# Softmax times V on one core: a third split load, the check of the values between passes, and the verdict in the last pass alone

## The chip, the core and the metric

The kernel runs on one core of one Trainium2 chip. The core has a matrix engine (TensorE, PE in the profile, with its weight loads listed as PEld), a vector engine (VectorE, DVE), an activation engine (ScalarE, ACT), a general engine (GpSimd, POOL) and an engine that here only issues transfers (SyncE, SP). Sixteen DMA engines move data between HBM and the on-chip buffers. The metric is the device time of one execution in microseconds (us); less is better.

## What is computed

```python
# scores: (8, 12, 1024, 1024) float32, v: (8, 12, 1024, 64) float32
scores_max = np.max(scores, axis=-1, keepdims=True)
attn = np.exp(scores - scores_max)
attn = attn / (np.sum(attn, axis=-1, keepdims=True) + 1e-8)
return np.matmul(attn, v).astype(np.float32)
```

There are 96 heads. A head has a 1024x1024 matrix of scores (4.19 MB) and a 1024x64 matrix of values (0.26 MB), and gives a 1024x64 result (0.26 MB).

## The kernel before

**Passes.** A loop (L423) runs 24 times; the text counts these passes from 0 to 23. A pass takes four heads as two pairs, `k` = 0 and `k` = 1, with n0 = 4 times the number of the pass. A pair lies in one buffer of scores, `s_bufs[k]`, of 128 partitions by 16 "rows" `r` by 1024 float32: 8.39 MB. So there are 32 rows in a pass; the text numbers them 0 to 31 across both pairs.

**One row.** ACT takes the exponential without subtracting the maximum (L377), two rows in one instruction, or one row for the last eight rows of a pass (`late`), into one of eight float16 buffers `p_nat`. PE transposes the row in eight blocks (L390; called T0 to T31 here) into PSUM, in one of two buffers `psT` of two rows each. DVE copies the transposed rows back to SBUF: two rows at a time (L402, 128x2048; called p0 to p11 here), or one row (L398) for the last eight. PE multiplies the copied row with the values and with a column of ones (L152; F0 to F31), so that the sum of the row comes out beside the product. After three rows DVE takes the reciprocals of the sums into `seen` (L132) and multiplies (L140). The product of a row is put `LAG` = 3 rows behind its transposition (L409), and PE's order is fixed by hand (`in_line`).

**Values.** `v_sb` holds the values of four heads in float32. POOL spreads them into the float16 tile `vones` (L248): those of pair 0 after that pair's last product (L163), those of pair 1 at the end of the pass (`last`, L352).

**Checks.** Because the maximum is not subtracted, the kernel checks that the fast way was allowed. `watch_v` (L257) takes the largest magnitude of `vones` on DVE, once a pass, behind the copy of row 7 (L404), and folds it into `fits` (L269). `judge` (L281) runs at the end of each pass (L414): two small reductions fold `seen` (L285, L286), two small operations make `right` (L289, L292), PE counts the good partitions with one matmul (L297), and DVE writes `count` (L301). After the loop every engine reads `count` (L430), and if it is not 128 the slow `general` runs (L434). It does not run in the profiled execution.

**Transfers.** All are issued by SP on one queue, in an order fixed by hand (`queue`). A pass issues: the load of pair 0 of the next pass (`load_first`, L225: three conditional instructions, of which only the one for the whole pair runs, except in pass 22, where the two halves run), the store of pair 0 (L170), and then, in an arm of `last`, the load of pair 1 of the next pass (L219), the store of pair 1 and the load of the next values (L238). A load into a buffer of scores waits until ACT has read the rows that it overwrites. The load of pair 1 is one transfer of 8.39 MB in passes 0 to 21; in pass 22 it is cut into seven (4, 4, 3, 2, 1, 1, 1 rows). Pass 23 only stores its results (`end`, L180).

**`last`** (L347) is a set of branches on n0, which every engine executes, whether it has work in them or not.

Of the kernel before, what the change touches and what calls it, by code (L numbers as in the profile page):

```python
# [26 lines left out]
def kernel(  # L27
# [6 lines left out]
    nc = tc.nc  # L34
# [155 lines left out]

    stores = []
    writers, users = {}, {}
    watches = []

    def apart(a, b, reason="stores of two heads are disjoint"):
        tc.declare_no_dep(a.ins, b.ins, across_iterations=True, reason=reason)
# [47 lines left out]
    def spread_v(k):  # L244

        for t in range(T):
            for s in range(S):
                spread = nc.gpsimd.tensor_copy(  # L248
                    out=vones[s * Q : (s + 1) * Q, k, :, t, 0:D].rearrange(
                        "i (h l) d -> i h l d", l=L  # L250
                    ),
                    in_=v_sb[(k * T + t) * Q : (k * T + t + 1) * Q, :, s],
                )
                for watch in watches:
                    apart(spread, watch, "products in between")

    def watch_v(behind):  # L257

        watch = nc.vector.tensor_reduce(  # L259
            out=most,  # L260
            in_=vones[:, :, :, :, 0:D].rearrange("p k c t d -> p k (c t) d"),
            axis=mybir.AxisListType.XYZ,
            op=ALU.max,
            apply_absolute_value=True,
        )
        after(watch, behind)
        watches.append(watch)
        for bound, op in ((V_MIN, ALU.is_ge), (V_MAX, ALU.is_le)):
            nc.vector.scalar_tensor_tensor(  # L269
                out=fits, in0=most, scalar=bound, in1=fits, op0=op, op1=ALU.mult  # L270
            )
# [6 lines left out]
    most, fits, right = small("most"), small("fits"), small("right", FP16)  # L278
    nc.gpsimd.memset(fits, 1.0)

    def judge(bank):  # L281

        n = K * R
        part = small("part")
        nc.vector.tensor_reduce(out=seen[:, 0:1], in_=seen[:, 0 : n + 1], axis=X, op=ALU.min)  # L285
        nc.vector.tensor_reduce(  # L286
            out=seen[:, n + 1 : n + 2], in_=seen[:, 1 : n + 2], axis=X, op=ALU.max
        )
        nc.vector.scalar_tensor_tensor(  # L289
            out=part, in0=seen[:, n + 1 : n + 2], scalar=1.0, in1=fits, op0=ALU.is_le, op1=ALU.mult  # L290
        )
        nc.vector.scalar_tensor_tensor(  # L292
            out=right, in0=seen[:, 0:1], scalar=1.0 / SUM_MAX, in1=part, op0=ALU.is_ge, op1=ALU.mult
        )
        cell = bank[0:1, G * M : G * M + 1]
        in_line(
            nc.tensor.matmul(  # L297
                out=cell, lhsT=right[:], rhs=vones[:, 0, 0, 0, D : D + 1], start=True, stop=True
            )
        )  # L300
        nc.vector.tensor_copy(out=count[:], in_=cell)  # L301

    def general():

        s_rows = scores.rearrange("b h (r p) j -> (b h r) p j", p=P)
        v_rows = v.rearrange("b h (c p) d -> (b h) p c d", p=P)
        o_rows = out.rearrange("b h (r p) d -> (b h r) p d", p=P)
        row, p_row, pt = (s_bufs[0][:, r, :] for r in range(3))
        v1 = s_bufs[0][:, 3, 0 : C * (D + 1)].rearrange("p (c m) -> p c m", m=D + 1)
        out_row = s_bufs[0][:, 4, 0:D]  # L310
        lift, den = small("lift"), small("den")
        nc.gpsimd.memset(s_bufs[0][:, 3, 0 : C * (D + 1)], 1.0)
        half = SK // 2
        with tc.For_i(0, BH * C, 1, iteration_sync="reg_based") as n:
            nc.sync.dma_start(out=row, in_=s_rows[bass.ds(n, 1)].rearrange("o p j -> (o p) j"))
            nc.sync.dma_start(
                out=v1[:, :, 0:D], in_=v_rows[bass.ds(n // C, 1)].rearrange("o p c d -> (o p) c d")
            )
            nc.vector.tensor_reduce(out=lift, in_=row, axis=X, op=ALU.max, negate=True)
            nc.scalar.activation(out=p_row, in_=row, func=EXP, bias=lift[:])  # L320
            for c in range(C):
                at = c * P % half
                nc.tensor.transpose(
                    out=psO_bufs[c * P // half][:, at : at + P],
                    in_=p_row[:, c * P : (c + 1) * P],
                    identity=ident32[:],
                )
            for h in range(2):
                nc.scalar.copy(out=pt[:, h * half : (h + 1) * half], in_=psO_bufs[h][:, 0:half])
            for c in range(C):  # L330
# [12 lines left out]
            nc.sync.dma_start(  # L343
                out=o_rows[bass.ds(n, 1)].rearrange("o p d -> (o p) d"), in_=out_row
            )

    def last(n0):  # L347

        before = queued[-1:]
        k = K - 1  # L350
        with tc.If(n0 < BH - AHEAD) as cmp:
            spread_v(k)  # L352
            with tc.If(n0 < BH - 2 * AHEAD) as cmp2:
                queued[:] = before
                load(k, (n0 + (AHEAD + T * k)) % BH)
                store(n0, k)
                load_v((n0 + 2 * AHEAD) % BH)
            with cmp2.Else():
                queued[:] = before
                load(k, BH - T, (4, 4, 3))  # L360
                store(n0, k)
                load(k, BH - T, (2, 1, 1, 1), 11)
        with cmp.Else():
            queued[:] = before
            end()

    def heads(n0):

        for k in range(K):
            st = dict(psO=[take(psO_bufs) for g in range(GROUPS)])  # L370
            for r in range(R):
                late = k == K - 1 and r >= R // 2
                if r % EB == 0:
                    p_nat, psT2, pt2 = take(p_bufs), take(psT_bufs), take(pt_bufs)
                    rows = 1 if late else EB
                    for g in range(0, EB, rows):
                        exp = nc.scalar.activation(  # L377
                            out=p_nat[:, g : g + rows, :].rearrange(
                                "p r (x v) -> p x r v", v=Q * L
                            ),  # L380
                            in_=s_bufs[k][:, r + g : r + g + rows, :].rearrange(
                                "p r (i x l) -> p x (r i) l", i=Q, l=L
                            ),
                            func=EXP,
                        )
                        rewrite(p_nat, exp)
                p_row = p_nat[:, r % EB, :].rearrange("p (h q l) -> p h l q", q=P, l=L)
                psT, pt = psT2[:, r % EB, :], pt2[:, r % EB, :]
                for c in range(C):
                    turned = nc.tensor.transpose(  # L390
                        out=psT[:, c * P : (c + 1) * P],
                        in_=p_row[:, c // L, c % L, :],
                        identity=ident16[:],
                    )
                    in_line(turned)
                    other_bank(psT2, r % EB, turned)
                if late:
                    copy = nc.vector.tensor_copy(out=pt, in_=psT)  # L398
                    rewrite(pt2, copy)
                    other_bank(psT2, r % EB, copy)  # L400
                elif r % EB == EB - 1:
                    copy = nc.vector.tensor_copy(out=pt2[:], in_=psT2[:])  # L402
                    rewrite(pt2, copy)
                if k == 0 and r == R // 2 - 1:  # L404
                    watch_v(copy)
                if r == R - 1 and k < K - 1:
                    load_first(n0)
                pending.append((n0, k, r, pt, st))
                if len(pending) > LAG:  # L409
                    finish(pending.pop(0))  # L410
        while pending:
            finish(pending.pop(0))
        last(n0)
        judge(st["psO"][-1])  # L414

    assert BH % AHEAD == 0 and BH >= 2 * AHEAD and SK == Q * S * C and K == 2
    load_v(0)
    for k in range(K):
        load(k, T * k, (R // 2, R // 2) if k == 0 else (R,))
    for k in range(K):  # L420
        spread_v(k)
    load_v(AHEAD)
    with tc.For_i(  # L423
        0, BH, AHEAD, iteration_sync="reg_based"
# [41 lines left out]
```

## Time and profile before

| what | value |
|---|---|
| time, median of 3 runs | 1070.16 us (1069.1 to 1070.58) |
| the profiled execution | 1069.46 us |
| its span, first to last instruction | 1067.5 us |
| PE / DVE / ACT / POOL busy | 793.6 / 768.8 / 737.3 / 239.2 us |
| moved by DMA | 453.06 MB, mean 424 GB/s |
| packets of the one large queue | 98.6% of 16 engines' span |
| mean granted TensorE clock | 0.897 |

The profiled execution is 0.7 us below the median and 1.96 us above its own span. Busy time is an average over stretches with different limits: an engine that is busy for 74% of the span may still set the pace for a short stretch. All times of day below are in us from the start of the span. In the profile's groups, "PE psO <- vones,pt" is a product, "PE psT <- ident,p_nat" a transposition, "DVE pt <- psT" a copy; a wait is put down to the releaser that came last by the profile, and where that engine had long been done it was another.

### The profile page before, as it was taken

To read this page: it belongs to the slowest core of one execution; us is meant where nothing else is said; L and a number is where in the kernel's file an instruction comes from. 1 tells how busy PE (TensorE), PEld (TensorE's weight loads), DVE (VectorE), ACT (ScalarE), POOL (GpSimd) and SP (SyncE) were. 2 spreads that over 40 slices of the span, in tenths; PEclk is the share of its full clock that TensorE was granted. 3 is DMA by queue.
4 is the path that set the end of the run, shared out by engine and by line. 5 is a ranking of instruction groups with operands and counts; after the bars stand their busy time and mean duration, and the time that the engine had idled before them with its cause. 6 is when DMAs were issued, how large, how long until landed. Compare 5 with 4: busy or idle time off the path is not lost.

```text
span 1067.5 us, 32791 instructions
## 1 busy us (share of the span) xinstructions
PE 793.6 (74%) x12312; PEld 757.7 (71%) x12312; DVE 768.8 (72%) x1539; ACT 737.3 (69%) x504; POOL 239.2 (22%) x399
## 2 busy tenths in 40 slices
PE   2578768786786777867878668776786777866887
PEld 2578668686686776867768668776686777866877
DVE  1578767696686866867769667785686866867788
ACT  3567568666686576856867668667686586756893
POOL 3031131211311203113121131221311303113121
PEclk9889889898898988989989889898898988989899
DMA  9999999999999999999999999999999999999993
GB/s 393 441 438 413 422 462 413 452 413 431 453 413 452 426 419 449 417 433 446 440 425 449 425 423 452 413 428 456 413 452 413 431 453 413 452 410 434 432 429 151
DMA packets 18580, 453.06 MB, mean 424 GB/s; under 512 B 2064, under 2 KB 2192, under 8 KB 8720
## 3 DMA queue, kind: packets, MB, share of 16 engines
q1 hardware_dynamic: 18576, 452.99, 98.6%
q8 instruction: 4, 0.07, 0.0%
HBM read 637.53 MB, written 25.17 MB: 621 GB/s over the span
## 4 chain that ended last, share of the span: by engine, by line
DMA 58%; ACT 27%; issue 6%; PE 3%; PEld 2%; DVE 2%; ACTq 1%; SPq 0%; PEldq 0%; DVEq 0%
DMA s_nat<-in_scores_dram 58%; ACT p_nat L377 26%; PE psO L152 1%; PEld L390 1%; PE psT L390 1%; DVE pt L402 1%; PEld L152 1%; ACTq L377 1%; DVE most L259 0%; ACT L377 0%; DVE pt L398 0%; SPq L219 0%; ACTq L423 0%; DVE seen L132 0%; DVE out_sb L140 0%
## 5 line engine op out<-in xcount | busy, mean ns | idle before, releaser
L377 ACT ACTIVATE p_nat<-s_nat 128x2048 f16<-128x2048 f32 (+1 forms) x480 | 706.5, 1557 | 118.9 <-PE psO L152 42.5
L390 PE MATMUL psT<-ident,p_nat 128*128 128x128 f16 x6144 | 505.4, 232 | 166.2 <-ACT p_nat L377 166.2
L390 PEld LDWEIGHTS <-p_nat 128*128 128x128 f16 x6144 | 425.1, 118 | 176.0 <-ACT p_nat L377 176.0
L402 DVE COPY pt<-psT 128x2048 f16<-128x2048 f16 x288 | 352.4, 1224 | 261.5 <-PE L390 165.2
L152 PE MATMUL psO<-vones,pt 128*128 128x130 f16 x6144 | 486.6, 223 | 62.9 <-DVE fits L269 40.4
L152 PEld LDWEIGHTS <-pt 128*128 128x128 f16 x6144 | 387.8, 99 | 84.7 <-DVE pt L402 55.6
L248 POOL CAST vones<-v_sb 32x512 f16<-32x512 f32 x392 | 238.5, 608 | 813.4 <-PE psT L390 318.6
L140 DVE TENSOR_TENSOR out_sb<-psO,seen 64x192 f32<-64x192 f32 (+1 forms) x576 | 191.8, 333 | 18.0
L377 ACT ACT_TABLE_LOAD x24 | 30.8, 1283 | 195.4 <-DMA s_nat<-in_scores_dram 178.5
L398 DVE COPY pt<-psT 128x1024 f16<-128x1024 f16 x192 | 123.5, 685 | 2.3
L259 DVE TENSOR_REDUCE most<-vones 128x1 f32<-128x2048 f16 x24 | 54.9, 2286 | 0.7
L132 DVE RECIPROCAL seen<-psO 128x3 f32<-128x3 f32 (+1 forms) x288 | 49.3, 171 | 2.8 <-PE L390 1.4
L297 PE MATMUL psO<-vones,right 128*1 128x1 f16 x24 | 3.9, 164 | 41.0 <-DVE right L292 41.0
L297 PEld LDWEIGHTS <-right 128*1 128x1 f16 x24 | 1.9, 79 | 45.3 <-DVE right L292 45.3
L301 DVE CAST count<-psO 1x1 int32<-1x1 f32 x24 | 3.5, 146 | 6.2 <-PE psO L297 6.2
L269 DVE SCALAR_TENSOR_TENSOR fits<-most,fits 128x1 f32<-128x1 f32 x48 | 7.4, 155 | 0.0
L289 DVE SCALAR_TENSOR_TENSOR part<-seen,fits 128x1 f32<-128x1 f32 x24 | 5.3, 220 | 0.8
L285 DVE TENSOR_REDUCE seen<-seen 128x1 f32<-128x33 f32 x24 | 4.5, 188 | 0.8
L292 DVE SCALAR_TENSOR_TENSOR right<-seen,part 128x1 f16<-128x1 f32 x24 | 3.9, 162 | 0.8
L286 DVE TENSOR_REDUCE seen<-seen 128x1 f32<-128x33 f32 x24 | 4.2, 177 | 0.0
L77 DVE MEMSET vones<- 128x64 f16 x1 | 0.1, 112 | 0.8 <-PEq L450 0.8
L74 DVE CAST ident<-ident 128x128 f16<-128x128 f32 x1 | 0.2, 227 | 0.4 <-POOL ident masks.py:199 0.4
(8 smaller groups left out, 1.1 us busy)
## 6 DMA issues: line engine op xcount, KB each, us to landing
s_nat<-in_scores_dram SPq DMA_DIRECT2D x50, 4096.0 KB, 18.7
v_sb<-in_v_dram SPq DMA_DIRECT2D x24, 1024.0 KB, 22.2
out_dram<-out_sb SPq DMA_DIRECT2D x47, 512.0 KB, 16.8
s_nat<-in_scores_dram SPq DMA_DIRECT2D x2, 2048.0 KB, 22.8
s_nat<-in_scores_dram SPq DMA_DIRECT2D x1, 1536.0 KB, 27.5
s_nat<-in_scores_dram SPq DMA_DIRECT2D x3, 512.0 KB, 20.8
s_nat<-in_scores_dram SPq DMA_DIRECT2D x1, 1024.0 KB
s_nat<-in_scores_dram SPq DMA_DIRECT2D x47, 28.4
```

Of the source, the lines that this page charges most:

```text
L132: nc.vector.reciprocal(out=recip, in_=psO[:, :, D : D + 1])
L140: nc.vector.tensor_tensor(out=out_bufs[k][part, g * G : g * G + rows, :], in0=psO[part, :, t * N : t * N + D], in1=recip[part].to_broadcas ...
L152: product = nc.tensor.matmul(out=st["psO"][g][:, i * M : (i + 1) * M], lhsT=pt[:, c * P : (c + 1) * P], rhs=vones[:, k, c].rearrange("p t ...
L248: spread = nc.gpsimd.tensor_copy(out=vones[s * Q : (s + 1) * Q, k, :, t, 0:D].rearrange("i (h l) d -> i h l d", l=L), in_=v_sb[(k * T + t) ...
L259: watch = nc.vector.tensor_reduce(out=most, in_=vones[:, :, :, :, 0:D].rearrange("p k c t d -> p k (c t) d"), axis=mybir.AxisListType.XYZ, ...
L269: nc.vector.scalar_tensor_tensor(out=fits, in0=most, scalar=bound, in1=fits, op0=op, op1=ALU.mult)
L289: nc.vector.scalar_tensor_tensor(out=part, in0=seen[:, n + 1 : n + 2], scalar=1.0, in1=fits, op0=ALU.is_le, op1=ALU.mult)
L297: nc.tensor.matmul(out=cell, lhsT=right[:], rhs=vones[:, 0, 0, 0, D : D + 1], start=True, stop=True)
L377: exp = nc.scalar.activation(out=p_nat[:, g : g + rows, :].rearrange("p r (x v) -> p x r v", v=Q * L), in_=s_bufs[k][:, r + g : r + g + ro ...
L390: turned = nc.tensor.transpose(out=psT[:, c * P : (c + 1) * P], in_=p_row[:, c // L, c % L, :], identity=ident16[:],)
L398: copy = nc.vector.tensor_copy(out=pt, in_=psT)
L402: copy = nc.vector.tensor_copy(out=pt2[:], in_=psT2[:])
```

## The change

The check of the values reads `v_sb` (as loaded) in place of `vones`, and stands once before the loop and then in `last`, behind the second spreading, in the arm of passes 0 to 22. `judge` is cut in two: `fold`, the two small reductions, stays at the end of each pass ahead of `last`; the rest moves into the arm of the last pass. The load of pair 1 that pass 21 issues, for pass 22, is cut into two halves by one more branch. In the last two rows of a pass the products follow their transpositions one row closer. The slow `general` issues its transfers from ACT in place of SP.

```diff
-    def watch_v(behind):
-
-        watch = nc.vector.tensor_reduce(
+    def watch_v():
+
+        nc.vector.tensor_reduce(
             out=most,
-            in_=vones[:, :, :, :, 0:D].rearrange("p k c t d -> p k (c t) d"),
-            axis=mybir.AxisListType.XYZ,
+            in_=v_sb[:].rearrange("p h s l d -> p (h s l d)"),
+            axis=X,
             op=ALU.max,
             apply_absolute_value=True,
         )
-        after(watch, behind)
-        watches.append(watch)
...
-    def judge(bank):
+    def fold():
 
         n = K * R
-        part = small("part")
         nc.vector.tensor_reduce(out=seen[:, 0:1], in_=seen[:, 0 : n + 1], axis=X, op=ALU.min)
         nc.vector.tensor_reduce(
             out=seen[:, n + 1 : n + 2], in_=seen[:, 1 : n + 2], axis=X, op=ALU.max
         )
+
+    def judge(bank):
+
+        n = K * R
+        part = small("part")
...
-    def last(n0):
+    def last(n0, bank):
 
         before = queued[-1:]
         k = K - 1
         with tc.If(n0 < BH - AHEAD) as cmp:
             spread_v(k)
+            watch_v()
             with tc.If(n0 < BH - 2 * AHEAD) as cmp2:
-                queued[:] = before
-                load(k, (n0 + (AHEAD + T * k)) % BH)
-                store(n0, k)
-                load_v((n0 + 2 * AHEAD) % BH)
+                with tc.If(n0 < BH - 3 * AHEAD) as cmp3:
+                    queued[:] = before
+                    load(k, (n0 + (AHEAD + T * k)) % BH)
+                    store(n0, k)
+                    load_v((n0 + 2 * AHEAD) % BH)
+                with cmp3.Else():
+                    queued[:] = before
+                    load(k, BH - 2 * AHEAD + T * k, (R // 2, R // 2))
+                    store(BH - 3 * AHEAD, k)
+                    load_v(BH - AHEAD)
             with cmp2.Else():
                 queued[:] = before
                 load(k, BH - T, (4, 4, 3))
-                store(n0, k)
+                store(BH - 2 * AHEAD, k)
                 load(k, BH - T, (2, 1, 1, 1), 11)
         with cmp.Else():
             queued[:] = before
             end()
+            judge(bank)
...
-                if k == 0 and r == R // 2 - 1:
-                    watch_v(copy)
                 if r == R - 1 and k < K - 1:
                     load_first(n0)
                 pending.append((n0, k, r, pt, st))
-                if len(pending) > LAG:
+                while len(pending) > (LAG - 1 if late and r >= R - EB else LAG):
                     finish(pending.pop(0))
         while pending:
             finish(pending.pop(0))
-        last(n0)
-        judge(st["psO"][-1])
+        fold()
+        last(n0, st["psO"][-1])
...
     for k in range(K):
         spread_v(k)
+    watch_v()
     load_v(AHEAD)
```

The rest of the diff takes away the list `watches` and its declarations, and writes `nc.scalar.dma_start` for `nc.sync.dma_start` three times in `general`.

More of the change, by code (lines that the diff above doesn't have):

```diff
@@ L192 @@
     writers, users = {}, {}
-    watches = []
     def apart(a, b, reason="stores of two heads are disjoint"):
@@ L247, in spread_v @@
             for s in range(S):
-                spread = nc.gpsimd.tensor_copy(
+                nc.gpsimd.tensor_copy(
                     out=vones[s * Q : (s + 1) * Q, k, :, t, 0:D].rearrange(
@@ L253, in spread_v @@
                 )
-                for watch in watches:
-                    apart(spread, watch, "products in between")
-    def watch_v(behind):
-        watch = nc.vector.tensor_reduce(
+    def watch_v():
+        nc.vector.tensor_reduce(
             out=most,
-            in_=vones[:, :, :, :, 0:D].rearrange("p k c t d -> p k (c t) d"),
-            axis=mybir.AxisListType.XYZ,
+            in_=v_sb[:].rearrange("p h s l d -> p (h s l d)"),
+            axis=X,
             op=ALU.max,
@@ L314, in general @@
         with tc.For_i(0, BH * C, 1, iteration_sync="reg_based") as n:
-            nc.sync.dma_start(out=row, in_=s_rows[bass.ds(n, 1)].rearrange("o p j -> (o p) j"))
-            nc.sync.dma_start(
+            nc.scalar.dma_start(out=row, in_=s_rows[bass.ds(n, 1)].rearrange("o p j -> (o p) j"))
+            nc.scalar.dma_start(
                 out=v1[:, :, 0:D], in_=v_rows[bass.ds(n // C, 1)].rearrange("o p c d -> (o p) c d")
@@ L342, in general @@
             nc.scalar.mul(out_row, psO_bufs[2][:, 0:D], den[:])
-            nc.sync.dma_start(
+            nc.scalar.dma_start(
                 out=o_rows[bass.ds(n, 1)].rearrange("o p d -> (o p) d"), in_=out_row
             )
-    def last(n0):
+    def last(n0, bank):
         before = queued[-1:]
@@ L412, in heads @@
             finish(pending.pop(0))
-        last(n0)
-        judge(st["psO"][-1])
-    assert BH % AHEAD == 0 and BH >= 2 * AHEAD and SK == Q * S * C and K == 2
+        fold()
+        last(n0, st["psO"][-1])
+    assert BH % AHEAD == 0 and BH >= 3 * AHEAD and SK == Q * S * C and K == 2
     load_v(0)
```

## The prediction

> **What bounds the kernel.** I read the page's slices of DMA first.
>
> ```profile
> DMA  9999999999999999999999999999999999999993
> ...
> q1 hardware_dynamic: 18576, 452.99, 98.6%
> ```
>
> All slices but the last are full. A pass moves 16.78 MB of scores and 1.05 MB each of values and results; ACT's passes start 43.6 us apart (897.34, 940.93, 984.56): 433 GB/s. Up to pass 21 the time is that of the bytes, and work on an engine costs nothing while transfers are queued. What a pass saves there is waited away at the next landing. So only the stretch behind the last landing that compute waits for can change: ACT's timeline finds it.
>
> ```profile
> 984.56 1.28 ACT L377 ACT_TABLE_LOAD   x1 [8.11 <-DMA s_nat<-in_scores_dram]
> 985.86 14.53 ACT L377 ACTIVATE p_nat<-s_nat 128x2048 f16<-128x2048 f32 x8
> 1005.11 14.90 ACT L377 ACTIVATE p_nat<-s_nat 128x2048 f16<-128x2048 f32 x12 [4.73 <-PE L390]
> 1020.04 1.28 ACT L377 ACT_TABLE_LOAD   x1
> 1021.33 24.57 ACT L377 ACTIVATE p_nat<-s_nat 128x2048 f16<-128x2048 f32 x15
> ```
>
> Pass 22 starts at a landing (984.56); pass 23 follows without one. The 4.73 us before 1005.11 are put down to PE, but that buffer's rows were transposed long before. The load of pair 1 was issued at 976.58, and the trace gives 28.4 us to landing: 1005.0. It is the landing. From there the chain of waits has almost only PE and DVE, up to the end. The last scores land at 1050.4 (issued 1029.58, 20.8 us), the last transposition is at 1058.5: compute is some 7 us late, which is the most that can be won.
>
> **Term 1: pass 22 up to its row 16.** The check and what follows, old (start, length, engine, line; in brackets idle time and what ended it):
>
> ```profile
> 997.80 2.29 DVE L259 TENSOR_REDUCE most<-vones 128x1 f32<-128x2048 f16 x1
> ...
> 1000.22 1.23 DVE L402 COPY pt<-psT 128x2048 f16<-128x2048 f16 x1
> ...
> 1001.50 0.63 PE L152 MATMUL psO<-vones,pt 128*128 128x130 f16 x8 [1.68 <-DVE fits L269]
> ...
> 1007.08 0.64 PE L390 MATMUL psT<-ident,p_nat 128*128 128x128 f16 x8 [0.84 <-ACT p_nat L377]
> ```
>
> Behind the check come p4, F8 and T16. The check holds up p4, and with it F8. Without it p4 starts behind T9 (ends 997.98), at about 998.2, and ends at 999.4; PE is free at 999.65, so F8 starts at 999.8, not 1001.50. Eight groups of 0.455 us (F8 to F11, T12 to T15) reach 1003.5, F12 1004.0, and T16 could follow: before, it had to wait for ACT until 1007.08. Here the split counts. At 433 GB/s half a pair takes 9.7 us, so the first half lands about 995.4, and ACT, done with pair 0 at 1000.4, goes straight on: its first rows of pair 1 are there at 1002.3. T16 moves to 1004.0, by **3.1 us**. Without the split it stays at 1007.08, and this term is nothing. From T16 on nothing shifts between engines: DVE had 1.08 us idle before 1008.74, then runs back to back, as does PE. F31 ends at 1021.4 (1024.48), the last multiplication at 1022.3 (1025.37).
>
> **Term 2: between pass 22 and pass 23.** Old:
>
> ```profile
> 1025.40 0.19 DVE L285 TENSOR_REDUCE seen<-seen 128x1 f32<-128x33 f32 x1
> ...
> 1026.20 0.16 PE L297 MATMUL psO<-vones,right 128*1 128x1 f16 x1 [1.71 <-DVE right L292]
> ...
> 1026.40 0.15 DVE L301 CAST count<-psO 1x1 int32<-1x1 f32 x1 [0.26 <-PE psO L297]
> ...
> 1027.26 3.02 PE L390 MATMUL psT<-ident,p_nat 128*128 128x128 f16 x30 [0.90 <-ACT p_nat L377]
> ...
> 1028.82 1.22 DVE L402 COPY pt<-psT 128x2048 f16<-128x2048 f16 x1 [2.27 <-PE L390]
> ```
>
> PE waited 1.71 us for the verdict, then spent 1.03 us on branches (its queue at L351, L353, L423), then transposed; DVE stood idle for 2.27 us. Now PE has no matmul of the verdict here: T0 at 21.3 + 1.0 = 1022.3, and T0 and T1 are done at 1023.3. The new wait is on DVE: the check sits ahead of p0, and F0, which waits for p0, and all of pass 23 queue behind. DVE: 1022.3 + 0.3 (fold) + 2.29 (check) + 0.3 (two operations on fits) = 1025.2, and 0.3 for branches (bounds 0 and PE's 1.0): p0 at 1025.5, not 1028.82. That is **3.3 us**, term 1 included. No row shows the check on float32. Bounds: 1.22 us, a copy of as many elements, and 4.6, twice 2.29 for twice the bytes: 1.1 us better or 2.3 worse. I take 2.29, the row of the same operation and count. [...] The check may run beside POOL's spreading (5.3 us); both only read `v_sb`, and the next load of values still waits for the later of the two, POOL.
>
> **Term 3: pass 23.** Old p3 to p4 took 3.67 us (1034.89 to 1038.56) with the check between; p4 to p8 took 7.47, 1.87 each. The check's going gives **1.8 us**, and since DVE never catches up behind it, it is kept. p0 to p3 took 6.07, of which PE ran cold: the granted clock was 0.50 from 1028 to 1031, with 12 matmuls per us, against 21 at 1.00. A cold stretch of 3.4 us costs 3.4 x (1 - 12/21) = 1.45 us. Warm, p0 to p3 takes 1.25 + 1.95 + 1.9 = 5.1: **0 to 1.0 us**. PE's new pauses are about 0.6, 1.0 and 2.3 us with 1.8 us of work between. I take half, 0.5. The row: PE went cold after 2.7 us in which only one small matmul ran. [...]
>
> Does a landing cap it? Landings follow in order: values 1008.8, first half of pair 0 1018.5, second 1028.2 (SP's issue at 1028.2 waits for it). Row 8's exponential is ready at 1030.2, PE wants it at 1030.6 or later. Row 31's is ready at 1051.4, and its copy is wanted at 1054.4. Neither binds, by 0.4 and 2 us.
>
> **What comes out at nothing.** The verdict in the last pass:
>
> ```profile
> 1060.52 0.69 DVE L398 COPY pt<-psT 128x1024 f16<-128x1024 f16 x1
> ...
> 1062.34 0.47 DVE L140 TENSOR_TENSOR out_sb<-psO,seen 64x64 f32<-64x64 f32 x2
> ...
> 1062.84 0.34 SPq L185 DMA_DIRECT2D out_dram<-out_sb  x1
> ...
> 1063.78 0.14 DVE L301 CAST count<-psO 1x1 int32<-1x1 f32 x1 [0.26 <-PE psO L297]
> ```
>
> It ends 1.1 us behind the last multiplication, the last store lands 2.3 us behind its issue (1065.1), and the end follows that. A branch ahead of the verdict, 0 to 1.0 us, is covered; without the cover it would cost itself. The closer products: the last copy (1060.52) waits for DVE's multiplication (to 1060.48), not for PE, so nothing (0.3 either way). The check before the loop ends by 8 us, before POOL's first spreading at 16.3. The extra branch and the second issue (0.3 us of SP) hide behind some 8 us of queued bytes. `general` never runs.
>
> **Sum.** 3.3 + 1.8 + 0.5 = 5.6 us off the profiled execution's 1069.46: 1063.9. That execution is 0.7 under the median of the runs, so the forecast on the median's scale is 1070.16 - 5.6 = 1064.6. With the check's bounds the win is 3.3 to 6.7, to which branches, clock and closer products add about 1 either way: 2.3 to 7.7, or 1062.5 to 1067.9.
>
> **Rivals.**
> - *A dearer boundary* (check near 4.6 us): 2.3 less, 1066.9. Against it: same engine, same count. 12%.
> - *The half brings nothing* (ACT's first rows wait for both parts): T16 stays, 3.1 less, 1067.7. For it: one instruction must serve three arms. Against it: pass 23's rows already follow their own parts. 10%.
> - *No difference*, within 0.2%: the end is set by landings after all, or two of these together. Against it: 7 us between landings and PE. 9%.
> - *Slower: SP is held in each pass.* The new branch adds counter work behind the load of values, where SP now runs five counter updates within 1.0 us (to 987.5). If one had to wait for that load's landing (1008.8), the next load of pair 0, now issued at 1000.5, would go out when the queue has run dry: some 2 us without bytes (a last store takes 1.9 to 2.3 to land) in each of 21 passes, 42 us, 1112. It decides from the point where SP is held past about 1006.5. Against it: today's updates wait for nothing so late. With smaller mishaps of the kind, 11%.
> - The forecast: 58%.
>
> A measurement of this kernel tells about 0.2% from no change, 2.1 us. Faster by more: 58 + 12 + 10 = 80%; same 9%; slower 11%. The range, 1062.4 to 1068.0, holds the first three.
>
> **What would show it.** Right: ACT without its pause before pair 1 in pass 22; T16 some 3 us earlier against pass 22's start; the check at 2.3 us with p0 right behind; p3 to p4 at 1.9; no matmul of L297 before the end. Wrong: starts of passes more than 43.6 apart; the pause still there; a check above 3 us; a cold stretch longer than 3.4 us in pass 23.

## The result, and the profile after

| what | before | after |
|---|---|---|
| median of 6 runs each | 1069.3 us (1069.1 to 1070.58) | 1065.99 us (1063.64 to 1066.35) |
| ratio of the times, with its 95% interval | | 0.996 [0.9947, 0.9973] |
| the profiled execution, its span | 1069.46, 1067.5 us | 1063.64, 1061.8 us |
| mean granted TensorE clock | 0.897 | 0.875 |

Faster, by 0.4%; the forecast was 1064.6 us and 1062.4 to 1068.0. The profiled executions are 5.8 us apart, where the sum of the terms said 5.6; the medians are only 3.3 apart. The changed kernel's times fall into two groups. In its 16 runs, from three sets, eight are at 1063.4 to 1064.1 and eight at 1065.9 to 1067.0, with none between. In each of them 1.73 to 1.89 us lie outside the span, so the 2.6 us between the means of the groups lie inside it. The profiled execution belongs to the lower group, and the median of a set goes with the group that holds most of its runs. The experiments come back to this.

The mean granted clock fell although the kernel became faster. It goes with the check's move: the profile of the run that moves the check alone has 0.873, those of the split alone and the verdict alone have 0.896 and 0.898.

The page's slices of DMA and its queue, after:

```profile
DMA  9999999999999999999999999999999999999995
...
q1 hardware_dynamic: 18720, 452.99, 99.1%
```

Still full to the end, and the passes up to 22 still start 43.6 us apart (897.44, 941.02, 984.67): the extra branch did not touch the stretch that the bytes set. Everything that follows is behind 984.67, the landing that starts pass 22.

ACT's timeline, after (start, length, engine, line, operation, count; in brackets idle time and what the profile names for its end):

```profile
985.97 18.14 ACT L384 ACTIVATE p_nat<-s_nat 128x2048 f16<-128x2048 f32 x10
1005.21 11.32 ACT L384 ACTIVATE p_nat<-s_nat 128x2048 f16<-128x2048 f32 x10 [1.11 <-PE psO L152]
1018.66 1.28 ACT L384 ACT_TABLE_LOAD   x1 [2.13 <-PE psO L152]
```

Ten exponentials now run in a row where there were eight: of the 4.73 us before 1005.11 a pause of 1.11 is left, and the first half of pair 1 (issued at 971.58, landed 23.9 us later) is used as soon as ACT is free. The pause that is left ends with the second half's landing (issued at 976.59, landed 28.5 us later, at 1005.1), though the next rows, 4 to 7 of the pair, are in the first half. One instruction serves all passes, and in pass 23 the second part of pair 1 begins with its row 4; that this is why it waits is read from the code, and was not tried. Pass 23 no longer follows without a pause: ACT is done 2.13 us before the first half of pair 0 is there. What was late on PE is now early on ACT.

PE's timeline, T16 of pass 22 (nothing in brackets: it did not wait; before, it started at 1007.08):

```profile
1003.09 0.61 PE L397 MATMUL psT<-ident,p_nat 128*128 128x128 f16 x8
```

DVE's timeline at the boundary between pass 22 and pass 23:

```profile
1021.81 2.28 DVE L256 TENSOR_REDUCE most<-v_sb 128x1 f32<-128x2048 f32 x1
1024.12 0.70 DVE L264 SCALAR_TENSOR_TENSOR fits<-most,fits 128x1 f32<-128x1 f32 x2
1025.43 2.36 DVE L409 COPY pt<-psT 128x2048 f16<-128x2048 f16 x2 [0.62 <-PE psT L397]
1028.92 1.23 DVE L409 COPY pt<-psT 128x2048 f16<-128x2048 f16 x1 [1.13 <-PE psO L152]
```

The check is the new head of this chain: 2.28 us, then its two small operations, then 0.62 us of idle time, then p0 at 1025.43. The time is put down to PE's transposition, but T0 and T1 had ended at 1023.0 (1021.92 plus 1.08): it is not PE that p0 waits for. The prediction had branches there; the trace does not show what it is. The last multiplication of pass 23 ends at 1057.14 (1062.81 before), and the span ends 4.66 us later, as it did before (4.69).

### The profile page after: what moved, and what is told of

It is laid out like the page before. It is cut to its first block, busy times and chain, and to the rows that moved or that the text cites. A ratio compares the mean times of both kernels' runs of the same rounds, so it can differ in the third digit from the quotient of the medians.

```text
span 1061.8 us, 33004 instructions
## 1 busy us (share of the span) xinstructions
PE 804.0 (76%) x12289; PEld 778.8 (73%) x12289; DVE 774.6 (73%) x1470; ACT 737.7 (69%) x504; POOL 239.0 (23%) x399
## 4 chain that ended last, share of the span: by engine, by line
DMA 58%; ACT 27%; issue 6%; PE 5%; DVE 1%; ACTq 1%; PEld 0%; SPq 0%; DVEq 0%
DMA s_nat<-in_scores_dram 58%; ACT p_nat L384 26%; PE psT L397 3%; PE psO L152 3%; ACTq L384 1%; DVE pt L409 1%; PEld L152 0%; ACT L384 0%; DVE most L256 0%; PEld L397 0%; DVE pt L405 0%; DVE out_sb L140 0%; SPq L218 0%; ACTq L429 0%; DVE seen L132 0%
## 5 line engine op out<-in xcount | busy, mean ns | idle before, releaser
L397 PE MATMUL psT<-ident,p_nat 128*128 128x128 f16 x6144 | 519.6, 236 | 226.1 <-ACT p_nat L384 224.9
L397 PEld LDWEIGHTS <-p_nat 128*128 128x128 f16 x6144 | 437.2, 120 | 238.2 <-ACT p_nat L384 238.1
L152 PE MATMUL psO<-vones,pt 128*128 128x130 f16 x6144 | 498.6, 227 | 26.3 <-DVE pt L405 17.7
L152 PEld LDWEIGHTS <-pt 128*128 128x128 f16 x6144 | 401.8, 101 | 39.1 <-DVE pt L405 21.9
L256 DVE TENSOR_REDUCE most<-v_sb 128x1 f32<-128x2048 f32 x24 | 54.6, 2277 | 4.7 <-DMA v_sb<-in_v_dram 4.7
L264 DVE SCALAR_TENSOR_TENSOR fits<-most,fits 128x1 f32<-128x1 f32 x48 | 15.2, 316 | 1.7
L296 PE MATMUL psO<-vones,right 128*1 128x1 f16 x1 | 0.2, 164 | 1.7 <-DVE right L291 1.7
L300 DVE CAST count<-psO 1x1 int32<-1x1 f32 x1 | 0.1, 145 | 0.3 <-PE psO L296 0.3
L288 DVE SCALAR_TENSOR_TENSOR part<-seen,fits 128x1 f32<-128x1 f32 x1 | 0.2, 160 | 0.1
## 6 DMA issues: line engine op xcount, KB each, us to landing
out_dram<-out_sb SPq DMA_DIRECT2D x47, 512.0 KB, 20.6
```

Source lines behind the costliest of these rows:

```text
L152: product = nc.tensor.matmul(out=st["psO"][g][:, i * M : (i + 1) * M], lhsT=pt[:, c * P : (c + 1) * P], rhs=vones[:, k, c].rearrange("p t ...
L256: nc.vector.tensor_reduce(out=most, in_=v_sb[:].rearrange("p h s l d -> p (h s l d)"), axis=X, op=ALU.max, apply_absolute_value=True,)
L264: nc.vector.scalar_tensor_tensor(out=fits, in0=most, scalar=bound, in1=fits, op0=op, op1=ALU.mult)
L397: turned = nc.tensor.transpose(out=psT[:, c * P : (c + 1) * P], in_=p_row[:, c // L, c % L, :], identity=ident16[:],)
```

## The experiments

"The changed kernel" is the kernel after; "profiled" means the one execution with a trace. "Cold" means a granted clock of 0.50, "warm" one of 1.00. The runs were taken in three sets, each with its own runs of the kernel before, at 1069.47, 1069.49 and 1070.28 us (medians). Nearly all of these lie between 1068.4 and 1070.8, so a difference between medians of less than 1 us says little.

### The parts alone

**Once more the changed kernel.** No edit.

> The changed kernel as it is, a second look. My account: the gain sits in passes 22 and 23 alone, so the passes up to 21 start 43.6 us apart and the last multiplication of DVE ends 4 to 6 us earlier than before against the landing that starts pass 22. The six times of the changed kernel lie in two groups, about 1063.7 and 1066.1 us. My theory for the 2.4 us between them: cold stretches of PE (granted clock 0.50) in pass 22 or 23, which cost up to 1.45 us for each 3.4 us and fall differently from run to run; this profile should show the clock at 0.50 for some 3 us more in the last two passes if its time is near 1066, and as in the first profile if it is near 1063.7. Rival: the two groups come from the transfers; then the landing that starts pass 22 is later by 2 us.

1064.02 us (1063.61 to 1066.29), ratio 0.9951 [0.9938, 0.9965]. One run of five is in the upper group. PE's timeline at the boundary:

```profile
1021.89 3.62 PE L397 MATMUL psT<-ident,p_nat 128*128 128x128 f16 x32 [1.16 <-DVE seen L279]
1026.85 0.62 PE L152 MATMUL psO<-vones,pt 128*128 128x130 f16 x8 [1.34 <-DVE pt L409]
```

The 32 transpositions took 3.62 us; at full clock 1.95 us are enough (as in the kernel with the check on ACT, below). PE ran cold from about 1021.9 to 1025.3 (granted clock 0.81 from 1020 to 1023, 0.62 to 1026, 1.00 from there). F0, which waits for p0, started at 1026.85, behind the cold stretch, so this stretch cost nothing.

**The split alone**, in the kernel before:

```diff
+                with tc.If(n0 < BH - 3 * AHEAD) as cmp3:
...
+                with cmp3.Else():
+                    queued[:] = before
+                    load(k, BH - 2 * AHEAD + T * k, (R // 2, R // 2))
```

> The kernel before with the split load of pass 21 alone. My theory (check, split and verdict each open one wait, and a wait opened alone only lets the next one bind): the check still holds up F8 until 1001.5, so row 16 can be transposed at about 1006.1 and not 1007.1: 1.0 us less than before, 0.5 to 1.3. Rival (ACT's pause of 4.7 us was the cost, so the split is the gain): 3 to 4 us less.

1067.8 us (1067.21 to 1068.49), ratio 0.9981 [0.9972, 0.999]: 1.7 less. More than expected, and not the rival's 3 to 4. The last multiplication of pass 22 came only 0.5 us earlier (1024.84 to the fold's start), since the check still held up p4 and F8. The rest goes with the clock: this execution has no cold stretch at the start of pass 23 (granted clock 1.00 from 1023 to 1035), where the kernel before has one of 3.4 us (0.83 from 1027 to 1028, 0.50 to 1031, 0.96 to 1032), and from the fold's start to p3 it took 8.54 us instead of 9.49.

**The check moved alone**: `watch_v` reads `v_sb` and stands in `last`; no split, and the verdict in each pass, now ahead of `last`.

```diff
             spread_v(k)
+            watch_v()
...
-                if k == 0 and r == R // 2 - 1:
-                    watch_v(copy)
...
+        judge(st["psO"][-1])
         last(n0)
-        judge(st["psO"][-1])
```

> The kernel before with the check of the values moved alone: read from the values as loaded, at the end of each pass behind the verdict. My theory: in pass 22 nothing is won, since row 16 still waits for its landing; at the boundary the check (2.3 us) and its two operations queue behind the verdict and ahead of the first copy, which comes 1 to 2 us later than before; in pass 23 p3 to p4 shrinks from 3.7 to about 2.0: -0.5 to +1.0 us in all, no clear difference. Rival (the check in the middle was the cost, and is free at the boundary): 1.8 to 3.5 us less.

1070.41 us (1070.25 to 1071.75), ratio 1.0009 [1.0, 1.0018]: no gain, or a loss of 0.9. The profile (1071.5, one of the slower runs) shows why it is not even nought. PE reached row 16 early and stood there for 3.27 us until the landing (busy for 1.82 and 0.91 us in the two stretches of 3 us from 1002 to 1008); then it was cold (clock 0.68, 0.50 and 0.69 in the three stretches of 3 us from 1005 to 1014), and p8 came at 1009.89 instead of 1008.74. The pass ended 2.5 us later than before, and p0 of pass 23 came at 1033.28.

**The verdict moved alone**: `fold` in each pass, `judge` in the last.

```diff
             end()
+            judge(bank)
...
-        last(n0)
-        judge(st["psO"][-1])
+        fold()
+        last(n0, st["psO"][-1])
```

> The kernel before with the verdict moved into the last pass alone (two small reductions stay). My theory: without the small matmul PE starts pass 23 about 1.7 us earlier, and the pause of 2.7 us that let its clock fall shrinks to about 1 us; nothing else stands ahead of the first copy, so it comes 2.0 to 2.5 us earlier, and all of pass 23 with it: 2.0 to 3.4 us less. Rival (the verdict hides behind the branches, and the first copy waits for the landing of the scores): 0 to 0.5 us less.

1066.87 us (1066.66 to 1067.96), ratio 0.9973 [0.9962, 0.9985]: 2.6 less, in the range. Pass 22's end to p0 shrank from 3.42 to 1.26 us (1026.65 to 1027.91), counted from the fold's start. In this execution, the slowest of the seven, pass 22 itself ended 1.25 us later than before: PE stood 1.92 us before row 16 (busy for 1.08 us from 1005 to 1008) and was cold soon after (32 matmuls at a granted clock of 0.51 from 1008 to 1011).

The three parts alone sum to -1.7 + 0.9 - 2.6 = -3.4 us. Together they gave 3.3 by the medians, 5.8 between the profiled executions. The agreement of 3.3 with 3.4 is chance: the parts do not add up, as the next run shows.

**All but the split**: the changed kernel with one transfer for pair 1 in pass 22.

```diff
-                with tc.If(n0 < BH - 3 * AHEAD) as cmp3:
...
-                    load(k, BH - 2 * AHEAD + T * k, (R // 2, R // 2))
```

> The changed kernel with the split of pass 21's load undone. My theory: row 16 of pass 22 waits for its landing again (1007.1 and not 1003.1), and since PE now comes to that wait some 4 us early its clock falls while it stands, as in the run with the check moved alone, so that pass 22 ends 4 to 6 us later than in the changed kernel: 4 to 6 us more, about the time of the kernel before, though check and verdict stay moved. Rival (the three parts add up, each by what it gave alone): 1.7 us more.

1070.62 us (1068.7 to 1071.46), ratio 1.0007 [0.9998, 1.0016]: all the gain is gone. Alone the split was worth 1.7 us; taken from the three it costs 5.1 (1068.7 against 1063.64, the profiled executions, each the fastest of its kernel in that set) or 4.6 by the medians. PE's timeline shows the wait that the split takes away, and what comes behind it:

```profile
1007.13 1.04 PE L391 MATMUL psT<-ident,p_nat 128*128 128x128 f16 x8 [2.94 <-ACT p_nat L378]
```

T16 is where it was before the change (1007.08), as term 1 said. But now PE had been idle for 2.94 us instead of 0.84, and eight transpositions took 1.04 us instead of 0.64: the granted clock was 0.50 from about 1006.9 to 1010.3. So p8 came at 1009.93, later than the 1008.74 of the kernel before. Work that is done sooner, ahead of a wait that stays, makes the wait longer, and that cost more than it won. In the three executions in which PE stood before row 16 for 1.92, 2.94 and 3.27 us the clock fell there or soon after; in the kernel before, with 0.84 us, it did not (1.00 from 1006 to 1012).

### The boundary

**Without the check at the end of pass 22.** The values of the last pass are not checked here.

```diff
             spread_v(k)
-            watch_v()
             with tc.If(n0 < BH - 2 * AHEAD) as cmp2:
+                watch_v()
```

> The changed kernel without the check at the end of pass 22: the values of the last pass are not checked. It prices the check at the one boundary that no landing covers. My theory: DVE is free for the first copy at 1022.9 and not 1025.4, but four copies later row 8 waits for the second half of pair 0, which lands at 1028.2 and whose exponential is ready at 1030.2, only 0.7 us before PE took it: 0.3 to 1.0 us less than the changed kernel. Rival (DVE sets the pace of the whole last pass): 2.5 to 3.0 us less.

1062.62 us (1062.45 to 1063.05), ratio 0.9932 [0.9918, 0.9945]. The profiled execution is 0.6 under the changed kernel's. p0 comes 1.5 us earlier (1023.89), p4 only 0.5 (1032.75 against 1033.27). Two things stand in between. PE was cold for 3.4 us from about 1023.6 (granted clock 0.61 from 1023 to 1026, 0.82 to 1029), so p0 to p3 took 6.71 us instead of 5.60. And T8 needs the second half of pair 0 and its exponential, which started at 1028.54. In the run with the check on ACT, where PE stood waiting, T8 started 1.96 us behind that exponential's start (1030.15 and 1028.19), so here it could not have come before about 1030.5 with a warm PE either (an estimate from these rows). In the changed kernel T8 started at 1030.89: the landing is the next bound, about 0.4 us behind the check. The upper group of times is gone.

**The same, with pair 0 of pass 23 in four parts**, to move that bound:

```diff
-        load(0, BH - AHEAD, (R // 2, R // 2), cond=(n0 == BH - 2 * AHEAD))
+        load(0, BH - AHEAD, (R // 4,) * 4, cond=(n0 == BH - 2 * AHEAD))
```

> As the run without the check at the end of pass 22 (the values of the last pass are not checked), and pair 0 of the last pass is loaded in four parts and not in two. My theory: the third quarter lands at 1023.4, so row 8 no longer waits, and the 2.5 us that the first copy is earlier stay to the end: 1.8 to 3.0 us less than the changed kernel. Rival (landings do not matter there): the same as the run without the check.

1170.21 us (1169.33 to 1172.2), ratio 1.0937 [1.0922, 1.0952]: 9% slower, and a complete miss. The waits of SP's queue have a row at the top that the changed kernel does not have at all (waited in total, times, longest):

```profile
SPq L218 <- DMA v_sb<-in_v_dram: 452.7, 22, 22.1
```

In each pass SP stands before the next load of pair 0 until the load of the values has landed, some 20 us. By then the queue has run dry (15 GB/s from 939 to 942, 655 in the 3 us before), and ACT's passes start 48.2 and 48.7 us apart instead of 43.6:

```profile
942.76 1.28 ACT L384 ACT_TABLE_LOAD   x1 [12.89 <-SPq L352]
...
990.92 1.28 ACT L384 ACT_TABLE_LOAD   x1 [12.73 <-SPq L352]
...
1039.64 1.28 ACT L384 ACT_TABLE_LOAD   x1 [13.12 <-SPq L352]
```

Pass 21 starts at 1039.64 instead of 941.27 (the run without the check): 98 of the 109 us between the two profiled executions, 4.8 us or a little more in each of some 20 passes. This is the prediction's slower rival, with its place and its wait, in a kernel that is one edit away from the run before it. A pass here has nine transfer instructions on its path (five conditional ones for pair 0, two stores, the load of pair 1 and the load of values), the changed kernel seven. The wait is shown, its reason is not.

**The check on ACT instead of DVE.** The verdict tests the sum of squares of a partition's values there, with tighter bounds, instead of the largest magnitude.

```diff
-        nc.vector.tensor_reduce(
-            out=most,
+        nc.scalar.activation(
+            out=square,
             in_=v_sb[:].rearrange("p h s l d -> p (h s l d)"),
-            axis=X,
-            op=ALU.max,
-            apply_absolute_value=True,
+            func=mybir.ActivationFunctionType.Square,
+            accum_out=most,
         )
...
```

> The changed kernel with the check of the values on ACT: the sum of their squares in one activation, and bounds on that sum, which are stricter than those on the largest magnitude. My theory: ACT stands 2.1 us before the landing that opens pass 23 (and 8 us in other passes), so the check costs nothing there; DVE keeps only two small operations at the boundary (0.7 us) and is ready for the first copy before PE is: as the run without the check, 1062.4 to 1063.2, with no times near 1066, since PE's pause at the boundary is short. Rival (the activation delays the first exponential of pass 23 by itself and a table load): 1064 to 1066.

1062.8 us (1062.71 to 1062.93), ratio 0.9933 [0.992, 0.9947]. It is the fastest version that still checks all values, 3.2 us under the changed kernel's median of the same set (0.6 under its fastest run), and none of its five runs is in the upper group. ACT's timeline:

```profile
984.58 18.14 ACT L385 ACTIVATE p_nat<-s_nat 128x2048 f16<-128x2048 f32 x10 [6.22 <-DMA s_nat<-in_scores_dram]
...
1016.33 1.90 ACT L256 ACTIVATE square<-v_sb 128x2048 bf16<-128x2048 f32 x1
1018.13 0.19 ACT L256 ACTIVATION_READ_ACCUMULATOR square<-v_sb 128x1 f32 x1
1018.57 7.32 ACT L385 ACTIVATE p_nat<-s_nat 128x2048 f16<-128x2048 f32 x4 [0.25 <-PE psO L152]
```

The check fills the 2.13 us in which ACT waited anyway. A second gain came unasked: in the timeline from 975 to the end ACT loads no table, where the changed kernel loads one at the start of each pass (24 times 1.28 us), and no load stands between a landing and the first exponential (984.58, not 985.97). In pass 22 that is waited away at the second half of pair 1 (PE stands for 1.09 us between 1005 and 1008). p0 of pass 23 starts at 1022.81, 2.6 us earlier, and most of that is waited away at two landings:

```profile
1029.49 0.74 DVE L140 TENSOR_TENSOR out_sb<-psO,seen 64x192 f32<-64x192 f32 x2 [1.89 <-DMA out_dram<-out_sb]
1030.15 0.64 PE L398 MATMUL psT<-ident,p_nat 128*128 128x128 f16 x8 [1.72 <-ACT p_nat L385]
```

PE waits for row 8. DVE's first normalisation of pass 23 waits 1.89 us for the store of pair 0 of pass 22 (in the changed kernel issued at 1008.89 and landed 20.6 us later), and p3 stands behind it. Both paths come to DVE's next reciprocal, at 1031.41, almost together: F5, which follows T8, is done at 1031.26, and that reciprocal starts 1.14 us behind p3's start, as the one before it does behind p2's. So a faster load of row 8 alone would have won almost nothing here (an estimate from these rows, not tried). 0.9 us is left at the end (1056.26 against 1057.14).

### The two groups of times

**The changed kernel again**, in the third set. No edit.

> The changed kernel as it is, a third look, beside the next three on the same chip. My theory of the two groups of times: they differ by where PE's cold stretches fall behind the boundary between passes 22 and 23. A stretch that ends before the first product of pass 23 (1026.8) is hidden; one that reaches past it costs about 1.3 us for each 3.4 us. So the profile shows a time near 1063.7 with no cold stretch past 1027, or a time of 1065 to 1066.3 with one that ends at 1030 or later. Rival: a time near 1066 without a cold stretch there.

1066.01 us (1063.41 to 1067.03), ratio 0.9961 [0.9947, 0.9975]: two runs in the lower group, three in the upper. The profile is of the lower group (1063.47) and has no cold stretch behind the start of pass 22.

**Fillers ahead of pass 22**: 90 matmuls whose results nothing reads at the end of each of the passes 0 to 21, to start pass 22 warm.

```diff
...
+                for _ in range(90):
+                    in_line(
+                        nc.tensor.matmul(
+                            out=bank[:, G * M + 2 : G * M + 122], lhsT=ident16[:],
+                            rhs=ident16[:, 0:120], start=True, stop=True,
+                        )
+                    )
...
```

> The changed kernel with 90 matmuls into unused columns of PSUM at the end of passes 0 to 21, about 5.5 us of PE while it waits for a landing, so that its clock stays at 1.00 at the start of pass 22. My theory: pass 22 starts faster by up to 0.9 us, but row 20 waits for the second half of its pair, which lands at 1005.2 (its transposition came right behind its exponential at 1007.1), so nearly nothing is left of it: 0 to 0.5 us less than the changed kernel's 1063.7. If the second group of times at 1066 comes from a longer cold stretch at the start of pass 22, it is gone; rival: it comes from elsewhere, and some of the times are near 1066 here too.

1064.62 us (1063.27 to 1065.64), ratio 0.9946 [0.9933, 0.996]. The mean clock rose to 0.943, the lowest times stayed where they were (1063.27), and p0 of pass 22 did not move (990.02 against 989.86). Against the best executions of the changed kernel, which are nearly warm there by themselves (clock at 1.00 from about 990.7 on in the first profile), the fillers win nothing, and a spread of 2.4 us stays: it does not come from the start of pass 22 alone. The profiled execution (1064.83) had a cold stretch of 6.8 us from about 1023 on (clock 0.50 to 1029, 0.86 from there to 1032), which delayed p2 from 1028.92 to 1030.17: 1.25 us.

**The old distance of the last products.**

```diff
-                while len(pending) > (LAG - 1 if late and r >= R - EB else LAG):
+                while len(pending) > LAG:
```

> The changed kernel with the products of the last two rows at the old distance behind their transpositions. My theory: the last copy waits for DVE's multiplication, not for PE, so nothing changes: within 0.3 us of the changed kernel. Rival (the closer products let the last multiplication start earlier): 0.5 to 1.0 us more.

1065.86 us (1063.66 to 1066.83), ratio 0.9956 [0.9943, 0.997]: one run in the lower group and four in the upper, so the closer products are worth nothing that can be told from these times. But its profile (1066.83, span 1065.1) is the one that caught the upper group. Busy time in stretches, changed kernel first (stretch, its length, busy time and count of PE, its weight loads, DVE, ACT, POOL; then granted clock, DMA share, GB/s):

```profile
1026.00:1029.00 3.00, 2.20 (x39) 2.23 (x40) 1.87 (x3) 1.98 (x2) 0.14 (x1) 1.00 1.03 437
1029.00:1032.00 3.00, 3.00 (x57) 3.00 (x55) 2.90 (x5) 3.00 (x3) 0.00 (x0) 1.00 0.99 422
```

and the old distance:

```profile
1026.00:1029.00 3.00, 1.58 (x16) 1.61 (x17) 2.36 (x2) 1.97 (x2) 0.71 (x2) 0.50 1.01 429
1029.00:1032.00 3.00, 3.00 (x30) 3.00 (x29) 0.94 (x1) 3.00 (x3) 0.00 (x0) 0.50 1.00 426
```

PE is busy throughout the second stretch in both, and does 57 matmuls in the one and 30 in the other. A busy PE is not a fast PE: the count and the clock tell it, the busy time does not. The cold stretch lasts 10.2 us here, from about 1023.2 to 1033.4 (clock 0.53 from 1023 to 1026, 0.50 to 1032, 0.76 to 1035). p0 starts 0.6 us later than in the changed kernel's profile (pass 22 ended that much later, the fold at 1022.23 against 1021.61; it started cold here until about 992.5, an estimate from p2 at 993.97: with the clock back at about 990.7 in the changed kernel's profile p2 came at 993.35, with 993.5 in the kernel before at 994.43), p0 to p3 takes 8.06 us instead of 5.60, and the end is 3.3 us later. So about 2.5 of the 3.3 us, nearly the 2.6 between the groups, are the cold stretch behind the boundary.

**Fillers at the boundary**: 24 such matmuls, in the arm of pass 22 alone.

```diff
             with cmp2.Else():
                 queued[:] = before
...
+                for _ in range(24):
+                    in_line(
+                        nc.tensor.matmul(
...
```

> The changed kernel with 24 matmuls into unused columns of PSUM at the end of pass 22 alone, about 1.4 us of PE in the pause before pass 23. My theory: they are hidden, since the first copy of pass 23 waits for the check on DVE, and they keep the clock up more often: 1063.4 to 1064.3 in most runs, fewer near 1066. Rival (the second group has another cause): as many near 1066 as without them, about 4 of 10.

1066.01 us (1065.7 to 1066.74), ratio 0.9963 [0.9949, 0.9976]: a miss by the times, 2 us over what was expected. The spans say something else. They lie at 1061.9 to 1062.8, where those of the changed kernel lie at 1061.6 to 1062.3 or at 1064.1 to 1065.3: with PE kept busy across the boundary (24 matmuls in 1.42 us, then the transpositions without a pause) the upper group is gone from the span, and the profile has no cold stretch in pass 23 (clock 1.00 from 1020 to 1038). What spoils the time is that 3.7 to 4.0 us lie outside the span in every run, where the other versions of the changed kernel have 1.7 to 2.0. Why this kernel has 2 us more there is open.

So the upper group is, in the main, a cold clock behind the boundary. That is shown for the one execution of that group with a trace, and supported by three kernels whose spans lost the group: two that shorten PE's pause there (no check: p0 1.5 us earlier; check on ACT: 0.65 us before F0 instead of 1.99) and one that fills it. The first of them still has a stretch of 3.4 us in its profile, so one of that length does not bring the group. What decides from run to run whether the clock falls, and whether for 3.4, 6.8 or 10.2 us, is not shown: in the changed kernel's first profile it stayed at 1.00 behind pauses of 0.74 and 1.24 us, in its second it fell behind 0.74 and 1.16.

## Why the prediction was right, step by step

The mechanism was right, each step happened at its place, and the changed execution that was profiled came out 0.2 us beside the sum. That closeness is in part luck: the terms did less well than their sum, and the profiled execution is of the lower group. By the medians 3.3 of the 5.6 us came. The forecast was counted from 1070.16; the kernel before measured 1069.3 over six runs, from which the same terms would have made 1063.7.

- **What bounds it.** Right: nothing moved ahead of 984.67, and the whole difference lies behind it.
- **Term 1**, 3.1 us at T16: 4.0 (1007.08 to 1003.09). The step from F8 to T16 was right (4.11 against 4.2). F8 itself came at 998.98 instead of 999.8, because the clock was back at full speed at about 990.7 in this execution (0.55 from 988 to 991, 1.00 from there) and at about 993.5 in the old one (0.50 from 988 to 991, 0.58 to 994). That part is luck: with the fillers at the boundary the cold start lasted to about 993.7 (0.54 from 991 to 994), in a kernel with the same work there, and pass 22 ended 1.3 us later. From T16 to the end of pass 22 the gain was 3.8 (1025.37 to 1021.57).
- **Term 2**, p0 at 1025.5: 1025.43. The check took 2.28 us, and so the old row's 2.29 on half as wide a type was the right row; the ends of 1.22 and 4.6 can go. Two terms were mis-sized: the operations on `fits` took 0.70 us, not 0.3 (316 ns each over all passes, 155 before), and the idle time before p0 was 0.62, not 0.3. These 0.7 us ate what pass 22 had won beyond the forecast.
- **Term 3**, 1.8 + 0.5: p3 to p4 took 2.24 us, so 1.43 was won and not 1.8. The 1.87 was a mean over copies with and without a normalisation between them, and p3 is one with (1.23 + 0.18 + 0.74 and small gaps). p0 to p3 took 5.60 and gave 0.47, next to the 0.5 that was taken, but by luck: the 0.5 stood for a PE that is cold for half of the stretch, and in this execution the clock was 1.00 throughout. The warm value of 5.1 was mis-sized: p1 to p2 took 2.35 us, with DVE idle for 1.13 of them until PE was ready, and p2 to p3 2.11, not 1.95 and 1.9. The cold stretch of the kernel before thus cost 0.47 us between p0 and p3 and not 1.0; the split alone, with a warm PE and the old order, took 5.61 there too. (The 12 and 21 matmuls per us are counts of windows 1 us long, in which a matmul at an edge counts twice; over 3 us they are 10.3 and 18.3, which makes 1.5 us of the 1.45.) The rest of the pass gave 0.4. With p0's 3.4 the sum is 3.39 + 0.47 + 1.43 + 0.38 = 5.67 at the last multiplication.
- **The clock is the step that was mis-sized.** It was priced at 0 to 1.0 us, from one stretch of 3.4 us; the half that was taken between these ends was the author's estimate. In the traces it is 0 long, or 3.4 and hidden before F0 (both in the changed kernel), or 6.8 (1.25 us, fillers ahead of pass 22), or 10.2 (some 2.5 us, old distance). On this account the median is 1065.99 and not 1063.6, and 1.4 above the forecast. "A cold stretch longer than 3.4 us in pass 23" was named as what would show it wrong. Two traces have one (fillers ahead of pass 22, old distance); by the times it is there in about half of the changed kernel's runs, which is argued and not shown.
- **Landings.** "Neither binds, by 0.4 and 2 us" was right by little. With the check gone the landing of row 8 binds after about 0.4 us, and of the 2.6 us that the check on ACT wins at p0, 0.9 reach the end. The landing of pair 0's store, which binds there at the same time, was not in the list.
- **What comes out at nothing.** Right for the verdict in the last pass (4.66 us behind the last multiplication, 4.69 before) and for the closer products, as far as the times tell.
- **The rivals.** The dearer boundary did not come: the check took 2.28 us and not 4.6. "The half brings nothing" was mispriced: it would not have left 1067.7 but, as the run without the split shows, no gain at all, and in the profile the clock falls to 0.50 during the longer wait at row 16 (2.94 us). The slower rival did not come in this kernel, but two more instructions bring it, at 4.8 us a pass and not 2.

## What to carry to other kernels

Parts of a change that open the same chain are not to be summed: each part alone runs into the wait that the other takes away, and here the halved load was worth 1.7 us alone and 5.1 with the rest. Look for the engine that has become idle at the new bound and give it the work that stands at the head of the chain: the check moved from DVE to ACT cost nothing there and won another 3.2 us of the median, mostly because the upper group is gone. Before a transfer is cut into more parts in a loop, look at what the issuing queue waits for in each pass.

## What the runs showed of the hardware

- The granted clock fell to 0.50 at the boundary behind pauses of PE of 0.74 and 1.16 us, for 3.4 us (the changed kernel's second profile), and of 0.74 and 1.05 us, for 10.2 us (the old distance); with the fillers ahead of pass 22 it fell there for 6.8 us. Eight matmuls then took 1.01 to 1.07 us instead of 0.61 to 0.64.
- Of `tensor_reduce` over 2048 elements, float32 took 2.28 us and float16 2.29.
- ACT's square with a running sum took 1.90 + 0.19 us over 2048 float32 elements, and no table load stood between it and the exponentials (none from 975 us to the end); in the changed kernel a table load of 1.28 us stood behind the landing at the start of each pass (24 loads).
- With five conditional loads instead of three in a pass, SP waited for another load's landing, 452.7 us in all.
